# Two order edges behind a pair by seven products in a streaming-encoder block

## The chip, the cores and the metric

The kernel runs on one core of one Trainium2 chip. The metric is the device time of one execution in microseconds; several runs are taken, and their median is compared. Durations of single instructions come from one further, profiled execution.

## The reference

One layer of a hybrid encoder block on 256 rows of width 4096, all in float32, with every weight read once from memory:

```
xn   = rms_norm(x)
proj = xn @ w_in                      # 4096 x 14336: q, k, v, z_a, a_c, g_c, z_c
y_a  = rms_norm(chunked_attention(q, k, v)) * silu(z_a)
y_c  = rms_norm(conv_module(a_c, g_c)) * silu(z_c)     # gate, 31 taps, layer norm, @ w_pw
h    = x + concat(y_a, y_c) @ w_out                    # 4096 x 4096
gate = sigmoid(rms_norm(h) @ w_ple_gate + b_ple_gate)  # 4096 x 4096
out  = rms_norm(h + gate * (p @ w_ple))
```

Nearly all the work is in the matrix products with w_in, w_out and w_ple_gate.

## The kernel before, in words

**Parts.** TensorE (PE) multiplies values of a shortened float32 type. So each operand is split into a high part (`wh`, `uh`, `xh`: the value cast to that type) and a low part (`wl`, `ul`, `xl`: the value less its high part), and one product of float32 quality is three matmuls: xh by wh, xl by wh, xh by wl. For a weight, ScalarE (ACT) makes the cast (L204 in `parts_of`) and VectorE (DVE) the subtraction (L205 in the same helper).

**Tiles and loops.** `mixed_product` (L377) makes the product of all 256 rows (two halves of 128) with two column blocks of 512, in four accumulators. It goes through the weight's rows in blocks of 128, two at a time: a pair. An order, given as text (L348 to L362), lists the pairs and how each is done. A plain pair takes its two weights as they are, 24 matmuls. A pair marked `*` or `+` is done by seven products (P1 to P7) in place of eight, as in Strassen's scheme, 21 matmuls; it needs sums of weight blocks besides. With the weights w0 (first) and w1 (second) of the pair these are:

- the first sums `ua` (L518 and L519 on DVE; with `+` DMAs make them), with their cast and low part (`pair_parts`, L335, which calls `parts_of` and so shows as `uh` at L204 and `ul` at L205),
- the second sums `ub` (L531 and L532 on DVE, in that order, since the second needs the first), with their cast and low part too. P6 and P4 need these and are the last two in the list of products (L543 to L552).

The first weight of such a pair is split in its first column block alone (512 elements a partition, the rest 1024). In many orders the second sums are written over the first (`ua<-ua,wt` in the profile), in others to a tile of their own (`ub`). A mark `-` means that the second weight's low part is made by ACT's negated copy (L215 and L217 in `high_and_minus`) and an accumulating DMA of GpSimd (L524, or L495 in a plain pair); its products wait in a list until the next pair.

**Order.** Each engine works through its own queue strictly as written. The program is traced in the order of the source, and a planner then writes each engine's queue: it takes, by an estimate of times, the instruction that is first in the source among those whose inputs it expects to be there. An instruction of the following pair so gets in front of one of this pair that is not ready in the estimate. `pin` (L89) keeps marked instructions in the source's order. `queued_behind` (L223) opens a block in which each instruction on an engine gets an edge to a given instruction of that same engine: it is put later in the queue. No semaphore is involved. Before the change it is used in one place, L520, for the first sums of a pair marked `+`.

**Stages.** `mixed_product` is called 24 times: four times for the convolution's gated input (`glu_conv`, L802), six times for queries, keys and values (`heads`, L1021), twice for w_pw, four times for the output gates (`gated`, L1126), four times for w_out (L1215), and four times for the last gate with w_ple_gate (L1256 and L1302), which the text calls the gate products. Other work (attention, the convolution's taps, the layer norm) is laid between the pairs with `fill`.

Of the kernel before, what the change touches and what calls it, by code (L numbers as in the profile page):

```python
# [25 lines left out]
def hybrid_block(  # L26
# [72 lines left out]
    def two_columns(w, kb, col, apart):  # L99

        rows = w[kb * P : (kb + 1) * P, :]
        return bass.AP(
            tensor=rows.tensor, offset=rows.offset + col,
            ap=[list(rows.ap[0]), [apart, 2], [1, NB]],
        )
# [76 lines left out]
    def fill(n):  # L182
        for _ in range(min(n, len(later))):
            later.popleft()()
# [11 lines left out]
    def part_tiles():  # L196
        return [wpool.tile([P, KC, NB], F32R, tag=tag, name=tag, bufs=3) for tag in ("wh", "wl")]

    def parts_of(wt, kc, tiles=None):
        if tiles is None:  # L200
            tiles = part_tiles()
        wh, wl = tiles
        made = (
            nc.scalar.copy(wh[:, :kc, :], wt[:, :kc, :]),  # L204
            nc.vector.tensor_tensor(  # L205
                wl[:, :kc, :], wt[:, :kc, :], wh[:, :kc, :].bitcast(F32), ALU.subtract
            ),
        )
        recent[:] = made
        return (wh, wl), made  # L210

    def high_and_minus(wt):

        wh = wpool.tile([P, KC, NB], F32R, tag="wh", name="wh", bufs=3)
        nc.scalar.copy(wh, wt)  # L215
        low = spool.tile([P, KC, NB], F32R, tag="stage", name="low")
        nc.scalar.activation(low, wh.bitcast(F32), AF.Identity, scale=-1.0)  # L217
        return wh, low

    recent = []  # L220

    @contextmanager
    def queued_behind(made):  # L223

        with ExitStack() as queued:
            for ins in made:
                queued.enter_context(tc.issue_after(ins.ins))
            yield
# [106 lines left out]
    def pair_parts(src):  # L335

        tiles = [upool.tile([P, 2, NB], F32R, tag=tag, name=tag) for tag in ("uh", "ul")]
        return parts_of(src, 2, tiles)[0]
# [38 lines left out]
    def mixed_product(  # L377
# [37 lines left out]
        def add(name, x, w2, n, final, kinds=range(3), then=lambda ins: None):  # L415

            for kind in kinds:
                a, b = ((x[0], w2[0]), (x[1], w2[0]), (x[0], w2[1]))[kind]
                made.append(
                    nc.tensor.matmul(  # L420
                        banks[name], a, b, start=name not in begun,
                        stop=final and ends[name] == n and kind == 2 and not (left and name in "P2 P3 P4"),
                    )
                )
                begun.add(name)
                then(made[-1])

        def block(kb, h):
            t = lhs[kb // 4]
            return [t[:, kb % 4, q, h * P : (h + 1) * P] for q in range(2)]  # L430

        def add_plain(n, k, wh, wl, **kw):
            pair = order[n][0]
            for j in range(2):
                for h in range(NH):
                    name = (("P2", "P3"), ("P4", "X"))[h][j]
                    add(name, block(2 * pair + k, h), (wh[:, j], wl[:, j]), n, k == 1, **kw)

        waiting = []

        def add_waiting(n):

            while waiting and waiting[0][0] <= n:
                waiting.pop(0)[1]()
# [26 lines left out]
        for n, (pair, seven, by_dma) in enumerate(order):  # L471
            if n < done:
                continue
            if ahead:
                ahead(pair)
            wts = []
            for k in range(2):
                wt = wpool.tile([P, 2, NB], F32, tag="w", name="wt")
                if seven == "+" and k == 0:
                    nc.sync.dma_start(wt[:, 0], w[2 * pair * P : (2 * pair + 1) * P, col : col + NB])  # L480
                else:
                    nc.sync.dma_start(wt, two_columns(w, 2 * pair + k, col, apart))
                wts.append(wt)
            sums_ahead(n)
            if n >= len(order) - n_left:
                for k in range(2):
                    tiles = left[2 * (n - len(order) + n_left) + k]
                    held.append((2 * pair + k, parts_of(wts[k], 2, tiles and tiles())[0]))
                fill(fills[n % len(fills)])
                continue  # L490
            if not seven:
                add_plain(n, 0, *parts_of(wts[0], 2)[0])
                if by_dma:
                    wh, low = high_and_minus(wts[1])
                    nc.gpsimd.dma_start(  # L495
                        low, two_columns(w, 2 * pair + 1, col, apart), accum_op=ALU.add
                    )
                    add_plain(n, 1, wh, low, kinds=range(2))
                    waiting.append((n + 1, partial(add_plain, n, 1, wh, low, kinds=(2,))))
                else:  # L500
                    add_plain(n, 1, *parts_of(wts[1], 2)[0])
                add_waiting(n)
                fill(fills[n % len(fills)])
                continue
            begins = not helper
            if begins:
                for name in ("P1", "P5", "P7", "P6"):
                    helper[name] = ps_tmp.tile([P, NB], F32, tag="tmp", name=f"acc_{name}")
                banks.update(helper)
            w0, w1 = wts  # L510
            plus = partial(nc.vector.tensor_tensor, op=ALU.add)
            before = list(recent)
            w0h, w0l = parts_of(w0, 1)[0]
            if seven == "+":
                ua = ub = sums[n]
            else:
                ua = ub = upool.tile([P, 2, NB], F32, tag="u", name="ua")
                plus(ua[:, 0], w0[:, 0], w0[:, 1])  # L518
                plus(ua[:, 1], w0[:, 1], w1[:, 1])  # L519
            with queued_behind(before if seven == "+" else ()):  # L520
                uah, ual = pair_parts(ua)
            if by_dma:
                w1h, w1l = high_and_minus(w1)
                nc.gpsimd.dma_start(  # L524
                    w1l, two_columns(w, 2 * pair + 1, col, apart), accum_op=ALU.add
                )
            else:
                w1h, w1l = parts_of(w1, 2)[0]
            if seven == "*" and not sums:
                ub = upool.tile([P, 2, NB], F32, tag="u", name="ub")  # L530
            plus(ub[:, 0], ua[:, 0], w1[:, 1])  # L531
            plus(ub[:, 1], ub[:, 0], w1[:, 0])  # L532
            ubh, ubl = pair_parts(ub)
            first = len(made)

            def s_of(i):
                if pair in places:
                    return places[pair][i]
                t, at = comb[pair] if isinstance(comb, dict) else (comb[pair // 4], pair % 4)
                return [t[:, at + i // 2, q, (i % 2) * P : (i % 2 + 1) * P] for q in range(2)]  # L540

            k0, k1 = 2 * pair, 2 * pair + 1
            add("P1", block(k0, 0), (w0h[:, 0], w0l[:, 0]), n, True)  # L543
            add("P5", s_of(1), (uah[:, 0], ual[:, 0]), n, True)
            add("P7", s_of(0), (uah[:, 1], ual[:, 1]), n, True)
            for name, x, j in (("P2", block(k1, 0), 0), ("P3", s_of(3), 1)):
                part = partial(add, name, x, (w1h[:, j], w1l[:, j]), n, True)
                part(kinds=range(2 if by_dma else 3))
                if by_dma:
                    waiting.append((n + 1, partial(part, kinds=(2,))))  # L550
            add("P6", s_of(2), (ubh[:, 0], ubl[:, 0]), n, True)
            add("P4", block(k1, 1), (ubh[:, 1], ubl[:, 1]), n, True)  # L552
            add_waiting(n)
            if begins and on_begin:
                on_begin()
            if begins:
                tc.add_manual_dep(
                    made[first].ins, last_transpose[0].ins.name,
                    mybir.DependencyInfo(mybir.DependencyClass.NoSync, mybir.DependencyReason.DATA),
                    reason="transposes before the helpers take their banks",  # L560
                )
            if n == last_seven:
                on_helpers(helper)
                after_sevens()
            fill(fills[n % len(fills)])
# [859 lines left out]
```

## Time and profile before

| | before |
|---|---|
| median of 3 runs | 2026.0 us (2025.92 to 2027.42) |
| the profiled execution's own time | 2025.85 us |
| its span, first to last instruction | 2024.1 us |
| ACT busy | 1257.1 us (62%) |
| idle time of ACT before `wh` at L204, ended by PE | 351.7 us |
| idle time of ACT before `uh` at L204, ended by L532 | 76.1 us (39.2 for `ub`, 36.9 for `ua`) |
| weight loads by DMA, 512 KB each, issue to landing | 4.2 to 4.9 us |

A row of a timeline gives the start and the duration in us, the engine, the line of the kernel, the operation, the tile written and the tiles read, the shape, a count where equal instructions are merged, and in brackets the engine's idle time before it with what ended it. Starts of PE's matmuls are recorded, their ends are modelled. The granted clock of TensorE was 0.998 over the span.

### The profile page before, as it was taken

The numbers are of one execution on the slowest core, as the hardware profiler recorded it, in microseconds if no ns is written. First come the engines' busy times: TensorE is split into PE (matmuls) and PEld (weight loads), VectorE is DVE, ScalarE is ACT, GpSimd is POOL, SyncE is SP. The second block draws the span as 40 slices with busy tenths as digits, with TensorE's granted clock in tenths as the row PEclk, the third lists the DMA queues.
The fourth block names the chain that finished last, engine by engine and source line by source line (L and its number), as shares of the span: only waits on it lengthen the run. The fifth ranks groups of instructions, "written<-read, shape, count | busy, mean of one in ns | idle before, by whom it ended". The sixth has DMA issues, their size and how long they took to land.

```text
span 2024.1 us, 26329 instructions
## 1 busy us (share of the span) xinstructions
PE 2006.7 (99%) x9043; PEld 1648.0 (81%) x9043; DVE 1926.9 (95%) x2771; ACT 1257.1 (62%) x1634; POOL 65.3 (3%) x71
## 2 busy tenths in 40 slices
PE   9999999999999999999999999999999999999997
PEld 7888888878888888788888888887888888888876
DVE  7999999899999999888999999999999999999998
ACT  7655555665666556776566676765766766656565
POOL 0000000000000000000000000000000000000000
PEclk9999999999999999999999999999999999999999
DMA  8788878679668877556677786876767766666765
GB/s 290 225 233 241 249 221 250 178 220 257 200 198 257 255 206 235 164 176 205 202 239 215 225 244 209 240 239 204 236 215 230 234 200 200 211 218 206 232 207 180
DMA packets 174193, 447.72 MB, mean 221 GB/s; under 512 B 14302, under 2 KB 17518, under 8 KB 174058
## 3 DMA queue, kind: packets, MB, share of 16 engines
q1 hardware_dynamic: 161952, 417.93, 63.8%
q0 software_dynamic: 11456, 27.27, 7.9%
q8 instruction: 71, 1.16, 0.2%
q10 hardware_dynamic: 650, 0.84, 0.1%
q14 instruction: 64, 0.52, 0.1%
HBM read 441.78 MB, written 4.19 MB: 220 GB/s over the span
## 4 chain that ended last, share of the span: by engine, by line
PE 89%; DVE 6%; issue 2%; DMA 1%; ACT 1%; POOLq 0%; POOL 0%; ACTq 0%; DVEq 0%; SPq 0%
PE acc L420 68%; PE acc_P L420 17%; DVE wl L205 2%; DMA wt<-in_w_in_dram 1%; PE tmp_ps L170 1%; DVE cv L787 1%; PE acc L237 1%; DVE ul L205 1%; PE tmp_ps L959 0%; PE tmp_ps L943 0%; PE tmp_ps L977 0%; ACT uh L204 0%; DVE cv L868 0%; ACT wh L204 0%; PE tmp_ps L982 0%
## 5 line engine op out<-in xcount | busy, mean ns | idle before, releaser
L420 PE MATMUL acc<-wh,big_t 128*128 128x512 f32 x4028 | 1240.3, 391 | 0.9 <-ACT big_t L156 0.4
L204 ACT CAST wh<-wt 128x1024 fp32r<-128x1024 f32 (+1 forms) x716 | 684.3, 965 | 493.8 <-PE acc L420 351.7
L420 PEld LDWEIGHTS acc<-wh,big_t 128*128 128x128 f32 x4028 | 753.3, 188 | 157.1 <-issue 1.3
L205 DVE TENSOR_TENSOR wl<-wt,wh 128x1024 fp32r<-128x1024 f32 (+1 forms) x716 | 788.8, 1113 | 33.0 <-ACT wh L204 27.5
L420 PE MATMUL acc<-wl,big_t 128*128 128x512 f32 x1958 | 756.4, 392 | 0.3 <-DVE wl L205 0.2
L420 PEld LDWEIGHTS acc<-wl,big_t 128*128 128x128 f32 x1958 | 367.2, 188 | 78.1 <-DVE wl L205 2.7
L204 ACT CAST uh<-ua 128x1024 fp32r<-128x1024 f32 x187 | 196.6, 1051 | 103.0 <-DVE ua L519 51.7
L205 DVE TENSOR_TENSOR ul<-ua,uh 128x1024 fp32r<-128x1024 f32 x187 | 228.1, 1220 | 6.9 <-ACT uh L204 4.2
L787 DVE SCALAR_TENSOR_TENSOR cv<-uT,dw,cv 128x255 f32<-128x255 f32 (+23 forms) x480 | 203.6, 463 | 1.1
L420 PE MATMUL acc_P<-uh,big_t 128*128 128x512 f32 x570 | 174.6, 391 | 0.1
L204 ACT CAST uh<-ub 128x1024 fp32r<-128x1024 f32 x99 | 104.2, 1053 | 47.9 <-DVE ub L532 39.2
L420 PEld LDWEIGHTS acc_P<-uh,big_t 128*128 128x128 f32 x570 | 106.0, 188 | 24.5 <-ACT uh L204 3.3
L205 DVE TENSOR_TENSOR ul<-ub,uh 128x1024 fp32r<-128x1024 f32 x99 | 120.8, 1220 | 0.8 <-ACT uh L204 0.5
L420 PE MATMUL acc_P<-ul,big_t 128*128 128x512 f32 x285 | 109.7, 392 | 0.2 <-DVE ul L205 0.2
L420 PE MATMUL acc<-uh,big_t 128*128 128x512 f32 x286 | 88.6, 390 | 0.0
L420 PE MATMUL acc_P<-wh,big_t 128*128 128x512 f32 x286 | 88.3, 389 | 0.0
L518 DVE TENSOR_TENSOR ua<-wt 128x512 f32<-128x512 f32 x112 | 76.9, 686 | 10.0 <-DMA wt<-in_w_in_dram 6.2
L519 DVE TENSOR_TENSOR ua<-wt 128x512 f32<-128x512 f32 x112 | 76.8, 686 | 2.7 <-DMA wt<-in_w_in_dram 1.7
L420 PE MATMUL acc_P<-uh,comb_t 128*128 128x512 f32 x228 | 70.3, 391 | 0.3 <-ACT uh L204 0.2
L532 DVE TENSOR_TENSOR ub<-ub,wt 128x512 f32<-128x512 f32 x99 | 68.1, 688 | 1.4
L531 DVE TENSOR_TENSOR ub<-ua,wt 128x512 f32<-128x512 f32 x99 | 67.8, 685 | 0.0
L420 PEld LDWEIGHTS acc_P<-ul,big_t 128*128 128x128 f32 x285 | 53.3, 188 | 13.9 <-DVE ul L205 3.0
(254 smaller groups left out, 1631.0 us busy)
## 6 DMA issues: line engine op xcount, KB each, us to landing
wt<-in_w_in_dram SPq DMA_DIRECT2D x416, 512.0 KB, 4.7
wt<-in_w_out_dram SPq DMA_DIRECT2D x128, 512.0 KB, 4.5
wt<-in_w_ple_gate_dram SPq DMA_DIRECT2D x128, 512.0 KB, 4.2
wt<-in_w_pw_dram SPq DMA_DIRECT2D x32, 512.0 KB, 4.9
ua<-in_w_in_dram SPq DMA_DIRECT2D x31, 512.0 KB, 4.3
ua<-in_w_in_dram POOLq DMA_DIRECT2D x31, 512.0 KB, 8.8
wt<-in_w_in_dram SPq DMA_DIRECT2D x31, 256.0 KB, 2.8
low<-in_w_in_dram POOLq DMA_DIRECT2D x12, 512.0 KB, 8.2
```

The costliest lines, as they stand in the source:

```text
L170: nc.tensor.transpose(pt[:, i * T + h * P : i * T + (h + 1) * P], src[:, h, b] if len(src.shape) == 4 else src[:, h, b * P : (b + 1) * P], ...
L204: nc.scalar.copy(wh[:, :kc, :], wt[:, :kc, :]),
L205: nc.vector.tensor_tensor(wl[:, :kc, :], wt[:, :kc, :], wh[:, :kc, :].bitcast(F32), ALU.subtract),
L237: nc.tensor.matmul(acc, a, b[:, k, :], start=kb == 0 and kind == 0, stop=kb == kblocks - 1 and kind == 2,)
L420: nc.tensor.matmul(banks[name], a, b, start=name not in begun, stop=final and ends[name] == n and kind == 2 and not (left and name in "P2 ...
L518: plus(ua[:, 0], w0[:, 0], w0[:, 1])
L519: plus(ua[:, 1], w0[:, 1], w1[:, 1])
L531: plus(ub[:, 0], ua[:, 0], w1[:, 1])
L532: plus(ub[:, 1], ub[:, 0], w1[:, 0])
L787: nc.vector.scalar_tensor_tensor(cv[:, i, PAD - k :], uT[:, i, : T + k - PAD], dw[:, b, k : k + 1], cv[:, i, PAD - k :], ALU.mult, ALU.add,)
```

## The change

Each pair by seven products now leaves two instructions behind in a list, `last_sums`: the second of its second sums (L532) and ACT's cast of the second sums. The pair that follows in the same product takes them out. Its first weight is split in a block queued behind the first of them, which puts an edge on its low part (DVE); its second weight is split in a block queued behind the other one, which puts an edge on its cast (ACT), and on the negated copy where the pair has the mark `-`. The issue of GpSimd's DMA stays outside the block. The edges are the same for a plain pair and a pair by seven products; the last three pairs of the very last product (`left`) get none. No operation is added or taken away.

```
-        waiting = []
+        waiting, last_sums = [], []
...
-            wts = []
+            wts, second_sums, sum_cast = [], last_sums[:1], last_sums[1:]
+            last_sums.clear()
...
             if not seven:
-                add_plain(n, 0, *parts_of(wts[0], 2)[0])
+                with queued_behind(second_sums):
+                    both = parts_of(wts[0], 2)[0]
+                add_plain(n, 0, *both)
                 if by_dma:
-                    wh, low = high_and_minus(wts[1])
+                    with queued_behind(sum_cast):
+                        wh, low = high_and_minus(wts[1])
...
                 else:
-                    add_plain(n, 1, *parts_of(wts[1], 2)[0])
+                    with queued_behind(sum_cast):
+                        both = parts_of(wts[1], 2)[0]
+                    add_plain(n, 1, *both)
...
-            w0h, w0l = parts_of(w0, 1)[0]
+            with queued_behind(second_sums):
+                w0h, w0l = parts_of(w0, 1)[0]
...
+            with queued_behind(sum_cast):
+                w1h, w1l = high_and_minus(w1) if by_dma else parts_of(w1, 2)[0]
             if by_dma:
-                w1h, w1l = high_and_minus(w1)
                 nc.gpsimd.dma_start(
                     w1l, two_columns(w, 2 * pair + 1, col, apart), accum_op=ALU.add
                 )
-            else:
-                w1h, w1l = parts_of(w1, 2)[0]
...
             plus(ub[:, 0], ua[:, 0], w1[:, 1])
-            plus(ub[:, 1], ub[:, 0], w1[:, 0])
+            last_sums.append(plus(ub[:, 1], ub[:, 0], w1[:, 0]))
             ubh, ubl = pair_parts(ub)
+            last_sums.append(recent[0])
```

## The prediction

> **What bounds the kernel now.** I read the page first, then busy time by stretch, then the timelines of VectorE (DVE), ScalarE (ACT) and TensorE (PE) around the pairs by seven products. Two rows of the page and one of the view by stretch:
>
> ```profile
> span 2024.1 us, 26329 instructions
> ...
> PE 2006.7 (99%) x9043; PEld 1648.0 (81%) x9043; DVE 1926.9 (95%) x2771; ACT 1257.1 (62%) x1634; POOL 65.3 (3%) x71
> ```
>
> ```profile
> 60.00:1992.00 1932.00, 1929.07 (x8663) 1585.48 (x8662) 1858.94 (x2655) 1198.56 (x1522) 62.54 (x61) 1.00 0.72 221
> ```
>
> In the last row the second number is the length, then busy PE, PEld, DVE, ACT, POOL, the granted clock, and DMA. PE is idle for 17.4 us of the span, but for only 2.93 us of the 1932 us between the start and the last tail. A busy end is modelled, so I also count a late start: products in a row start 0.23 us apart (430.03 and 430.26 below), and what exceeds that is lost. The change can only win these losses back, where they hang on the chain that it touches.
>
> That chain belongs to one pair by seven products: first of the second sums (L531), second of them (L532), ACT's cast of both (`uh`), DVE's low part (`ul`), then the last two products, P6 and P4. The change puts two instructions of the following pair behind it: on DVE the first weight's low part behind L532, on ACT the second weight's cast behind the sums' cast. Where the queue already runs so, nothing moves. The view of line 532 counts the pairs:
>
> ```profile
> L532 DVE TENSOR_TENSOR ub<-ub,wt x99: 677/686/694, 64.6 to 1980.7; 128x512 f32<-128x512 f32 x99
> L532 DVE TENSOR_TENSOR ua<-ua,wt x44: 672/684/697, 115.0 to 870.0; 128x512 f32<-128x512 f32 x44
> ```
>
> That is 143 pairs. Going through the timelines, I find the second weight's cast ahead of the sums' cast after 27 of them; these are the first and the last of the 27 casts:
>
> ```profile
> 64.27 1.04 ACT L204 CAST wh<-wt 128x1024 fp32r<-128x1024 f32 x1
> ```
>
> ```profile
> 1978.97 1.04 ACT L204 CAST wh<-wt 128x1024 fp32r<-128x1024 f32 x1
> ```
>
> In only 6 of these is the low part ahead of L532 as well. 20 of the 27 lie after 1740 us, in the gate products. So 116 of 143 places have the order already.
>
> **The change part by part.** Place A, third GLU product, DVE, ACT, PE:
>
> ```profile
> 427.44 0.69 DVE L518 TENSOR_TENSOR ua<-wt 128x512 f32<-128x512 f32 x1 [1.01 <-DMA wt<-in_w_in_dram]
> 428.05 0.68 DVE L531 TENSOR_TENSOR ua<-ua,wt 128x512 f32<-128x512 f32 x1
> 428.65 1.22 DVE L205 TENSOR_TENSOR wl<-wt,wh 128x1024 fp32r<-128x1024 f32 x1
> 429.79 0.68 DVE L532 TENSOR_TENSOR ua<-ua,wt 128x512 f32<-128x512 f32 x1
> ```
>
> ```profile
> 427.51 1.06 ACT L204 CAST wh<-wt 128x1024 fp32r<-128x1024 f32 x1 [0.98 <-PE acc_P L420]
> 430.50 1.04 ACT L204 CAST uh<-ua 128x1024 fp32r<-128x1024 f32 x1 [1.94 <-DVE ua L532]
> ```
>
> ```profile
> 430.03 0.39 PE L420 MATMUL acc<-wl,comb_x 128*128 128x512 f32 x1
> 430.26 0.39 PE L420 MATMUL acc<-wh,big_t 128*128 128x512 f32 x1
> 431.60 0.73 PE L420 MATMUL acc_P<-uh,comb_x 128*128 128x512 f32 x2 [0.95 <-ACT uh L204]
> 432.17 0.63 PE L420 MATMUL acc<-uh,big_t 128*128 128x512 f32 x2
> ```
>
> The low part of the following weight stands between the two sums; the sums' cast starts 0.03 us after L532 ends (429.79 + 0.68), and P6 starts 0.06 us after the cast ends. From 430.26 to 432.17 are three starts: 1.91 less 3 x 0.23 is 1.22 us lost. With the edge L532 starts at 428.65 and ends at 429.33, the cast runs 429.36 to 430.40, and P6 can start at 430.46, before its turn at 430.49. So 1.22 us come back. The price: the low part ends at about 430.5 instead of 429.87; its product is in none of these rows and is after P6 in the pair's own order, so I take nothing. The moved cast starts about 2.8 us later (427.51 to about 430.3); ACT sat idle for 1.94 us in front of the sums' cast, which covers it. Behind it only later casts wait, and they were to start once the sums' cast was over in any case.
>
> Place B, the fourth GLU product, has the same order:
>
> ```profile
> 606.68 1.22 DVE L205 TENSOR_TENSOR wl<-wt,wh 128x1024 fp32r<-128x1024 f32 x1
> 607.82 0.69 DVE L532 TENSOR_TENSOR ua<-ua,wt 128x512 f32<-128x512 f32 x1
> ```
>
> ```profile
> 608.91 0.39 PE L420 MATMUL acc<-wh,big_t 128*128 128x512 f32 x1
> 609.64 0.73 PE L420 MATMUL acc_P<-uh,comb_x 128*128 128x512 f32 x2 [0.34 <-ACT uh L204]
> 610.21 0.40 PE L420 MATMUL acc<-uh,big_t 128*128 128x512 f32 x1
> ```
>
> 1.30 less 0.69 is 0.61 us lost. L532 at 606.68 puts P6 1.14 us earlier, at 608.50, before its turn at 609.14: all 0.61 come back.
>
> Place C, second output product, where the following pair's second weight goes by DMA, and only ACT's order is concerned:
>
> ```profile
> 1434.76 0.69 DVE L532 TENSOR_TENSOR ub<-ub,wt 128x512 f32<-128x512 f32 x1
> ```
>
> ```profile
> 1435.46 1.06 ACT L215 CAST wh<-wt 128x1024 fp32r<-128x1024 f32 x1 [0.98 <-PE acc_P L420]
> 1436.42 1.05 ACT L204 CAST uh<-ub 128x1024 fp32r<-128x1024 f32 x1
> ```
>
> ```profile
> 1438.62 0.39 PE L420 MATMUL acc<-uh,big_t 128*128 128x512 f32 x1
> 1438.98 0.50 PE L420 MATMUL acc_P<-ul,big_t 128*128 128x512 f32 x1
> 1439.32 0.40 PE L420 MATMUL acc<-uh,big_t 128*128 128x512 f32 x1
> ```
>
> The sums are done at 1435.45, but ACT takes the weight first. Exchanged, the sums' cast runs from 1435.48, 0.94 us earlier, and their low part `ul`, for which PE waits at 1438.98, can follow it. PE lost 0.70 less 2 x 0.23, 0.24 us; I take it all back. The two casts only swap, so the negated copy behind them, and GpSimd's accumulating DMA that it releases, start when they did before: nothing, and at most one cast (1.06 us) if they do not, on a transfer whose product is deferred to the next pair. No other queue's DMA is moved.
>
> Place D, last gate product, with both orders inverted and the opposite effect:
>
> ```profile
> 1956.55 1.22 DVE L205 TENSOR_TENSOR wl<-wt,wh 128x1024 fp32r<-128x1024 f32 x1
> 1957.68 0.68 DVE L532 TENSOR_TENSOR ub<-ub,wt 128x512 f32<-128x512 f32 x1
> ```
>
> ```profile
> 1952.37 1.04 ACT L204 CAST wh<-wt 128x1024 fp32r<-128x1024 f32 x1
> ...
> 1958.47 1.05 ACT L204 CAST uh<-ub 128x1024 fp32r<-128x1024 f32 x1 [2.80 <-DVE ub L532]
> ```
>
> ```profile
> 1957.28 0.61 PE L420 MATMUL acc_P<-wh,big_t 128*128 128x512 f32 x2
> 1957.82 0.96 PE L420 MATMUL acc<-wl,big_t 128*128 128x512 f32 x3
> 1958.62 0.62 PE L420 MATMUL acc<-wh,big_t 128*128 128x512 f32 x2
> ```
>
> Here PE fills its time with the following pair: at 1957.82 it waits for exactly the low part that the change sends back (five starts in 1.34 us: 0.19 lost). After the change L532 takes 1956.55 to 1957.23 and the low part ends near 1958.4; the sums' cast is over at 1958.3, so the earliest product is P6 at 1958.35 in place of 1957.82: 0.5 us more. And the products with `wh` at 1958.62, of a cast made five microseconds before, now have it at 1959.3; P6 and P4 fill that time. Bounds: the 0.19 won, 0.5 lost; I take 0.2 lost, since PE's order is planned anew too. The gate product before has a place of this kind; I give it the same as an estimate. The other 22 places I set at nothing: some close a short loss, some lose a filler of PE as in D. Their bounds I put at 1.5 us either way in all, eight times the 0.19 of place D, as an estimate.
>
> Sum: 1.22 + 0.61 + 0.24 - 2 x 0.2 = 1.7 us. The profiled execution took 2025.85 us, 1.75 beyond its span; less 1.7 that is 2024.15. The median of the runs shown, 2026.0, is 0.15 above that execution, so the forecast for the median is 2024.3. That is 0.08%, under the 0.2% (4.05 us) that a measurement of this kernel can tell from no change.
>
> **The rivals.** *VectorE takes the gain back.* Won time is only kept if DVE follows:
>
> ```profile
> 432.00:540.00 108.00, 108.00 (x489) 89.01 (x488) 105.66 (x168) 61.78 (x74) 7.61 (x7) 1.00 0.87 251
> 1740.00:1916.00 176.00, 175.95 (x771) 143.55 (x770) 174.54 (x213) 106.11 (x128) 0.00 (x0) 1.00 0.67 214
> ```
>
> After place A, DVE is busy for 105.66 of 108 us: 2.34 us of slack for 1.22 us won, enough if it lies in the right place. In the gate products it is 1.46 us in 176. The change removes no DVE work, so if DVE binds, the sum is 0 and the median 2026.0. For it: these rows; against: at A it is DVE's order, not its amount, that PE waits for. The Trainium skill ("Perfetto Trace Analysis", Identifying the Most-Contended Engine) says that matmul busy time does not show how near PE is to its limit, and has it judged by the weight loads' busy share; by that rule PE has a fifth to spare and DVE is the bound, which gives this rival's time. The trace speaks against the rule here: products start every 0.23 us without a gap at 81% of weight loads.
>
> *The planner's new order closes more.* One early shift moves everything planned behind it; if every idle stretch of the 2.93 us closed, and as much again in late starts, it would be 5.9 us and 2020.1. For it: 27 places are spread over the kernel. Against: transposes and attention, which the change does not touch, share in that idle time.
>
> *Slower: loads come later.* Place A's first row shows DVE waiting 1.01 us for a weight's DMA; a weight buffer is free only once its cast and low part are done. A second cast that comes a cast later (1.06 us) frees it later; where no margin is left, DVE and then PE pay the 1.06. It decides from two such places on (2.1 against 1.7 won); with six of the 27 it is 6.4 - 1.7 = 4.7 us, 2030.7. Against: the low part, not the cast, is the last to read, and DVE's total is unchanged.
>
> *It does nothing*: the edges bind in none but the 27 places, and PE's order may absorb those too: 2026.0.
>
> **How the numbers follow.** Forecast (some 1 to 3 us won) 0.55; given back 0.17; nothing done 0.05; more closed 0.13; slower 0.10. Of the third, 0.10 lies beyond 4.05 us; of the fourth, 0.07. So faster 0.10, same 0.83, slower 0.07. The range goes from 2021.3 (1.5 from the unsized places and another 1.5 of replanning) to 2027.5 (the gain gone and 1.5 lost): about one in ten on either side.
>
> **What would show it.** Right: at A and B no idle time before `acc_P<-uh,comb_x`, with L532 straight behind L531 or after a sum; at C the cast `uh` ahead of L215; in no place a `wh` of the second weight ahead of the `uh`; ACT idle before `uh`, as long as before. Wrong: new PE waits after 1740 us for `wl` or `wh` of more than 0.5 us each, more DVE idle time at L518 that a weight's DMA ends, as place A's first row has it, or a span shorter by over 4 us, which would need places that I took for untouched.

## The result and the profile after

The changed kernel is slower by 0.15%, where a gain of 0.08% was forecast: median 2029.66 us (2027.06 to 2032.15, 22 runs) beside 2026.37 us of the kernel before (22 runs), ratio 1.0015, 95% interval 1.0008 to 1.0021. That is 1.6 to 4.3 us, near the least that such a comparison can tell from no change. Timed a second time, it gave 1.0013 (1.0004 to 1.0022). The profiled execution took 2028.23 us, 1.83 beyond its span. Of the later kernels, one run each of e5 (4338.92 us) and e8 (2222.42 us) was in a slow state and is left out of the ratios; all other runs are fast ones.

The page of the changed kernel, then its busy time by stretch (columns as in the prediction):

```profile
span 2026.4 us, 26338 instructions
...
PE 2006.3 (99%) x9043; PEld 1648.5 (81%) x9043; DVE 1927.4 (95%) x2771; ACT 1256.1 (62%) x1634; POOL 65.3 (3%) x71
```

```profile
60.00:1992.00 1932.00, 1926.80 (x8655) 1584.59 (x8654) 1858.40 (x2653) 1196.25 (x1521) 62.55 (x61) 1.00 0.72 220
...
1740.00:1916.00 176.00, 175.07 (x766) 142.83 (x765) 173.65 (x212) 105.41 (x127) 0.00 (x0) 1.00 0.67 213
```

The work is the same: 9043 products, 2771 instructions of DVE, equal busy times. PE's idle time between the start and the last tail grew from 2.93 to 5.20 us, and in the gate products (1740 to 1916) from 0.05 to 0.93. Eight products fewer fell into the first stretch, eight times 0.23 us.

For all later comparisons I sum PE's late starts over the whole trace: each start less the one before it, less the 0.2275 us of products in a row. Only excesses of more than about 0.02 us count, and a constant 5.5 us or so is in every sum; so differences of the sums are to be read, not the sums. The sum is 29.23 us before and 32.03 after. In every profile of this study the span is 1994.4 to 1995.0 us plus this sum, so it accounts for the difference of two spans to within 0.6 us: here the sums differ by 2.80 and the spans by 2.3.

**Place A after.** DVE, then PE. In this kernel the first sums are L525 and L526, the second sums L537 and L538 (before: L518, L519, L531, L532).

```profile
426.51 0.69 DVE L525 TENSOR_TENSOR ua<-wt 128x512 f32<-128x512 f32 x1 [0.76 <-DMA wt<-in_w_in_dram]
427.12 0.68 DVE L537 TENSOR_TENSOR ua<-ua,wt 128x512 f32<-128x512 f32 x1
427.80 0.69 DVE L526 TENSOR_TENSOR ua<-wt 128x512 f32<-128x512 f32 x1
428.41 0.69 DVE L538 TENSOR_TENSOR ua<-ua,wt 128x512 f32<-128x512 f32 x1
429.01 1.22 DVE L205 TENSOR_TENSOR wl<-wt,wh 128x1024 fp32r<-128x1024 f32 x1
```

```profile
429.36 0.39 PE L420 MATMUL acc<-wl,comb_x 128*128 128x512 f32 x1
430.28 0.72 PE L420 MATMUL acc_P<-uh,comb_x 128*128 128x512 f32 x2 [0.53 <-ACT uh L204]
430.85 0.63 PE L420 MATMUL acc<-uh,big_t 128*128 128x512 f32 x2
431.54 0.50 PE L420 MATMUL acc_P<-ul,comb_x 128*128 128x512 f32 x1
431.88 0.39 PE L420 MATMUL acc<-ul,big_t 128*128 128x512 f32 x1
```

The edge was obeyed: the low part `wl` stands behind L538. But L538 does not start at L537's end. The planner put L526 there, the second first sum of a later pair. And PE lost the filler `acc<-wh,big_t` that stood ahead of P6 at 430.26 before. From 429.36 to 431.88 are six starts: 2.52 less 6 x 0.23 is 1.14 us lost, against 1.22 before.

**Place B after**, DVE and PE:

```profile
606.50 0.69 DVE L526 TENSOR_TENSOR ua<-wt 128x512 f32<-128x512 f32 x1 [0.16 <-DMA wt<-in_w_in_dram]
607.11 0.69 DVE L538 TENSOR_TENSOR ua<-ua,wt 128x512 f32<-128x512 f32 x1
```

```profile
607.84 0.39 PE L420 MATMUL acc<-wl,comb_x 128*128 128x512 f32 x1
608.98 0.74 PE L420 MATMUL acc_P<-uh,comb_x 128*128 128x512 f32 x2 [0.76 <-ACT uh L204]
...
610.58 0.39 PE L420 MATMUL acc<-ul,big_t 128*128 128x512 f32 x1
```

The same newcomer, and it waits for its weight's DMA. Six starts in 2.74 us: 1.36 us lost, where 0.61 were to be won.

**Place C after**, ACT, then PE:

```profile
1437.07 1.05 ACT L204 CAST uh<-ub 128x1024 fp32r<-128x1024 f32 x1 [1.09 <-DVE ub L538]
1438.03 1.04 ACT L215 CAST wh<-wt 128x1024 fp32r<-128x1024 f32 x1
```

```profile
1439.67 0.62 PE L420 MATMUL acc_P<-uh,big_t 128*128 128x512 f32 x2
1440.12 0.39 PE L420 MATMUL acc_P<-ul,big_t 128*128 128x512 f32 x1
1440.35 0.62 PE L420 MATMUL acc<-uh,big_t 128*128 128x512 f32 x2
```

The two casts have changed places, and three starts in 0.68 us leave nothing lost.

**Place D after**, the last gate product, DVE, ACT and PE:

```profile
1956.04 0.68 DVE L537 TENSOR_TENSOR ub<-ua,wt 128x512 f32<-128x512 f32 x1
1956.64 1.21 DVE L205 TENSOR_TENSOR ul<-ua,uh 128x1024 fp32r<-128x1024 f32 x1
1957.77 0.68 DVE L538 TENSOR_TENSOR ub<-ub,wt 128x512 f32<-128x512 f32 x1
1958.38 1.21 DVE L205 TENSOR_TENSOR wl<-wt,wh 128x1024 fp32r<-128x1024 f32 x1
```

```profile
1958.56 1.05 ACT L204 CAST uh<-ub 128x1024 fp32r<-128x1024 f32 x1 [2.44 <-DVE ub L538]
```

```profile
1958.80 0.39 PE L420 MATMUL acc<-wh,big_t 128*128 128x512 f32 x1
1959.67 0.74 PE L420 MATMUL acc_P<-uh,big_t 128*128 128x512 f32 x2 [0.48 <-ACT uh L204]
1960.25 0.63 PE L420 MATMUL acc<-uh,big_t 128*128 128x512 f32 x2
1960.72 0.85 PE L420 MATMUL acc<-wl,big_t 128*128 128x512 f32 x3
```

L538 is not earlier here: this time the low part `ul` of the first sums took the freed place. P6 starts at about the time at which it did before (1959.77), but PE runs dry ahead of it: before, ten products with weights of following pairs stood between 1957.28 and P6, and now most of these are planned behind it, as the `wl` at 1960.72. Three starts in 1.45 us: 0.76 lost. The view of PE's waits from 1740 us on (us in all, times, the longest) shows it for the gate products as a whole:

```profile
PE acc_P L420 <- ACT uh L204: 1.4, 3, 0.5
PE acc L408 <- DVE wl L205: 0.5, 1, 0.5
```

Three waits, one in each of the last three gate products, and one at the start of the last product's remainder at 1994.67; the kernel before has no wait of PE in this window.

### The profile page after: what moved, and what is told of

Its sections match the earlier page's. It is cut to its first block, busy times and chain, and to the rows that moved or that the text cites. A ratio compares the mean times of both kernels' runs of the same rounds, so it can differ in the third digit from the quotient of the medians.

```text
span 2026.4 us, 26338 instructions
## 1 busy us (share of the span) xinstructions
PE 2006.3 (99%) x9043; PEld 1648.5 (81%) x9043; DVE 1927.4 (95%) x2771; ACT 1256.1 (62%) x1634; POOL 65.3 (3%) x71
## 4 chain that ended last, share of the span: by engine, by line
PE 86%; DVE 7%; issue 3%; DMA 2%; ACT 1%; SPq 0%; POOLq 0%; POOL 0%; ACTq 0%; DVEq 0%
PE acc L420 65%; PE acc_P L420 17%; DVE wl L205 3%; DMA wt<-in_w_in_dram 1%; DVE ul L205 1%; PE tmp_ps L170 1%; PE acc L237 1%; DVE cv L794 1%; ACT uh L204 0%; ACT wh L204 0%; DVE hc L184 0%; DVE ua L525 0%; DVE ub L537 0%; PE tmp_ps L966 0%; PE tmp_ps L950 0%
## 5 line engine op out<-in xcount | busy, mean ns | idle before, releaser
L525 DVE TENSOR_TENSOR ua<-wt 128x512 f32<-128x512 f32 x112 | 76.6, 684 | 9.4 <-DMA wt<-in_w_in_dram 5.8
L526 DVE TENSOR_TENSOR ua<-wt 128x512 f32<-128x512 f32 x112 | 76.6, 684 | 4.6 <-DMA wt<-in_w_in_dram 4.1
L538 DVE TENSOR_TENSOR ub<-ub,wt 128x512 f32<-128x512 f32 x99 | 68.0, 687 | 1.5
L537 DVE TENSOR_TENSOR ub<-ua,wt 128x512 f32<-128x512 f32 x99 | 67.6, 682 | 0.0
```

Of the source, the lines that this page charges most:

```text
L538: last_sums.append(plus(ub[:, 1], ub[:, 0], w1[:, 0]))
```

## The experiments

The late starts of all profiles, in us, beside medians of 11 runs where nothing else is said (the GLU products named are the third and fourth, with places A and B; the gate products are the last four):

| kernel | median | ratio (95% interval) | two GLU | gate | rest | sum |
|---|---|---|---|---|---|---|
| before (3 runs) | 2026.0 | | 9.15 | 3.48 | 16.61 | 29.23 |
| e12 before again | 2025.58 | 0.9999 (0.9991 to 1.0008) | 8.58 | 3.41 | 16.76 | 28.75 |
| after (22 runs) | 2029.66 | 1.0015 (1.0008 to 1.0021) | 9.16 | 5.10 | 17.77 | 32.03 |
| e13 after again | 2028.92 | 1.0013 (1.0004 to 1.0022) | 9.41 | 4.93 | 18.23 | 32.57 |
| e1 low part alone | 2027.31 | 1.0007 (0.9998 to 1.0016) | 8.79 | 4.28 | 17.18 | 30.25 |
| e2 cast alone | 2028.93 | 1.0010 (1.0001 to 1.0019) | 10.02 | 5.51 | 17.54 | 33.07 |
| e3 gate products alone | 2027.67 | 1.0001 (0.9992 to 1.0010) | 8.73 | 5.14 | 15.85 | 29.73 |
| e4 all but gate products | 2027.62 | 1.0003 (0.9994 to 1.0012) | 10.02 | 3.54 | 17.54 | 31.11 |
| e5 first sums too | 2025.65 | 0.9999 (0.9990 to 1.0008) | 7.21 | 5.58 | 15.72 | 28.51 |
| e6 two GLU products | 2025.15 | 0.9995 (0.9986 to 1.0004) | 7.36 | 3.41 | 16.94 | 27.70 |
| e7 three places | 2028.52 | 1.0011 (1.0003 to 1.0020) | 9.49 | 5.92 | 15.16 | 30.57 |
| e8 all but three places | 2028.08 | 1.0009 (1.0000 to 1.0018) | 12.57 | 2.39 | 17.12 | 32.09 |
| e9 first sums too, but three | 2023.63 | 0.9990 (0.9981 to 0.9999) | 7.28 | 2.43 | 18.26 | 27.98 |
| e10 two GLU and gate | 2024.28 | 0.9990 (0.9981 to 0.9999) | 8.08 | 2.44 | 16.82 | 27.34 |
| e11 first sums, later P6 | 2024.56 | 0.9996 (0.9987 to 1.0005) | 7.13 | 3.57 | 16.31 | 27.01 |
| e14 first sums alone | 2025.48 | 0.9993 (0.9984 to 1.0001) | 7.40 | 3.45 | 16.80 | 27.65 |
| e15 TensorE's order alone (5 runs) | 2033.76 | 1.0040 (1.0026 to 1.0053) | 9.33 | 10.50 | 16.31 | 36.14 |
| e16 middle alone | 2025.60 | 0.9996 (0.9988 to 1.0005) | 8.21 | 3.28 | 17.35 | 28.84 |

A ratio is to runs of the kernel before made beside that kernel, and it is not the quotient of two medians: e3's median is 1.7 us over that of the runs beside it (2025.99), at a ratio of 1.0001. The late starts are those of a single execution each.

**Halves of the change (e1 to e4).** One edge at a time, then both edges in one part of the kernel. e1 and e2:

```
-            wts, second_sums, sum_cast = [], last_sums[:1], last_sums[1:]
+            wts, second_sums, sum_cast = [], last_sums[:1], []
...
+            wts, second_sums, sum_cast = [], [], last_sums[1:]
```

> Only the edge on VectorE is kept (the following first weight's low part behind L532); the cast on ScalarE is free. Theory 1, the loss comes from the gate products, where the second cast may no longer come early and TensorE is planned without its fillers: the low part stood ahead of L532 in 6 places only, so within 1 us of the kernel before (2025.5 to 2027.5 where before is 2026.4). Theory 2, the loss comes from the low part moved back, for which TensorE waits, and from the sums of other pairs that take its place: most of the 3.3 us, 2028.5 to 2030.

> Only the edge on ScalarE is kept (the following second cast behind the cast of the sums). Theory 1: nearly the whole loss stays, 2 to 3.5 us over before, with waits of 0.6 us for the cast of the sums in the last three gate products. Theory 2: under 1 us over before.

e3 and e4, where `products_made` counts the calls of `mixed_product`:

```
+            if len(products_made) <= 20:
+                second_sums, sum_cast = [], []
...
+            if len(products_made) > 20:
+                second_sums, sum_cast = [], []
```

> Both edges in the four gate products alone. Theory 1: 1.8 us over before, what TensorE lost there in the profile after (4.45 us of late starts after 1740 us against 2.66). Theory 3, the loss is at the boundaries of products (the four output gates), where the plan came out otherwise by chance: within 0.7 us of before.

> Both edges everywhere but in the gate products. Theory 1: 0.5 to 1.5 us over before, from the boundaries of the output gates; the third and fourth GLU product gain nothing together. Theory 3: 2.5 to 3.5 us over before.

By time the four can't be told apart: their intervals overlap, and e1, e3 and e4 hold 1. The traces say more. Each edge alone makes new waits before P6 in the last two gate products (e1: 0.67 and 0.64 us idle; e2: 0.48 and 0.44), and e2 makes the third as well (0.45); so the loss there is not that of one of the edges alone. And e3, with the edges in the gate products alone, has all of their extra late starts (5.14), e4 none (3.54). In e3's own time this loss does not show (1.0001, 0.9992 to 1.0010).

**The first sums at A and B (e5, e6, e14).** Here the first sums of a pair are queued behind the preceding pair's second sums as well. In e5 that is added to the change everywhere; in e6 only the low-part edge and this one stay, in the two GLU products alone.

```
+                with queued_behind(second_last):
                     plus(ua[:, 0], w0[:, 0], w0[:, 1])
                     plus(ua[:, 1], w0[:, 1], w1[:, 1])
...
             last_sums.append(recent[0])
+            second_last[:] = last_sums[:1]
```

> The change, and besides it the first sums of each later pair by seven (L518, L519) queued behind the last second sums in the same product. Theory 1: in the third and fourth GLU product the freed place between L531 and L532 was taken by such a sum, which waits for its weight's DMA; with this edge L532 follows L531 there, the product P6 waits less than 0.3 us (0.69 to 1.45 and 0.41 to 0.92 in the profiles with the change), and the kernel is 1.5 to 2.5 us under the change, 0.5 to 1.5 over before. Rival, VectorE takes the gain back: the waits close and the time stays that of the change.

> The low part's edge and the edge on first sums in the third and fourth GLU product alone, no edge on a cast, nothing elsewhere. Theory 1: both waits for P6 (1.22 and 0.61 us lost before) go, 1 to 2 us under before. Rival, VectorE takes the gain back: within 0.5 us of before, with later waits in the attention that follows.

The waits before P6 are gone in both, at A and at B. PE of e5 at A:

```profile
429.00 0.61 PE L420 MATMUL acc_P<-uh,comb_x 128*128 128x512 f32 x2
429.55 0.50 PE L420 MATMUL acc_P<-ul,comb_x 128*128 128x512 f32 x1
429.89 0.64 PE L420 MATMUL acc<-uh,big_t 128*128 128x512 f32 x2
```

P6 follows the product before it without idle time, and three starts in 0.89 us leave 0.20 lost, not 1.14. At B a wait for the sums' low part `ul`, just behind, took the place of the one before P6. PE of e6 at B:

```profile
608.96 0.50 PE L422 MATMUL acc_P<-ul,comb_x 128*128 128x512 f32 x1 [0.25 <-DVE ul L205]
```

B loses 0.43 us in e5 and 0.52 in e6, where the two profiles of the kernel before lose 0.61 and 0.47: no gain beyond what these two differ by. Over the whole kernel e5 is level with the kernel before, e6 not clear of it (0.9995, to 1.0004), and e5's median is 4 us under that of the change (from different comparisons).

e14 then took the low-part edge away and left the kernel before with the first-sum edge alone, in these two products:

```
+            second_sums, sum_cast = [], []
+            if len(products_made) not in (5, 7):
+                second_last.clear()
```

> The kernel before with one edge only: in the third and fourth GLU products the first sums (L518, L519) are queued behind the second of the second sums; the low part and the cast are free. Theory 1 (the low part still stands between the two sums, and both edges are needed): a wait of 0.5 to 1.3 us before P6 at about 430 us and 0.2 to 0.6 at about 608 us, as in the kernel before, and the time within 1 us of it. Rival (the first sums alone are the cause): no wait at either place, and 1 to 2 us under the kernel before.

I expected that both edges were needed. At A that was wrong. DVE of e14, whose second sums are L543 and L544, and PE:

```profile
424.46 1.23 DVE L205 TENSOR_TENSOR ul<-ua,uh 128x1024 fp32r<-128x1024 f32 x1
425.72 0.69 DVE L543 TENSOR_TENSOR ua<-ua,wt 128x512 f32<-128x512 f32 x1
426.33 1.22 DVE L205 TENSOR_TENSOR wl<-wt,wh 128x1024 fp32r<-128x1024 f32 x1
427.47 0.68 DVE L544 TENSOR_TENSOR ua<-ua,wt 128x512 f32<-128x512 f32 x1
```

```profile
429.30 0.39 PE L421 MATMUL acc<-wl,comb_x 128*128 128x512 f32 x1
429.52 0.62 PE L421 MATMUL acc_P<-uh,comb_x 128*128 128x512 f32 x2
```

The low part still stands between the two second sums, and P6 is on time. What also held the chain up at A is in the first row that the prediction quotes of this place: the first sum at 427.44, ahead of the second sums, with 1.01 us of idle time for its weight's DMA. It belongs to a later pair, whose weight was not there; without it the first of the second sums starts 0.03 us after the work before it. Taking it out is enough: A loses 0.31 us in e14. Whether moving the low part alone would have been enough too, with nothing in its place, no run shows. At B, where that first sum had not waited, e14 still has 0.27 us idle before P6, and the kernels with the low-part edge besides (e5, e6, e9, e10) have none. There P6 did wait for the low part, as predicted, but the place loses as much with `ul` late. The two GLU products lose 7.40 us in e14 and 7.21 and 7.36 in e5 and e6; so nearly all that is won there is won at A, and by the first sums.

**The gate products (e7, e8, e11, e15).** e7 leaves both edges only behind the pair `6*` of the last three gate products; e8 takes out just these.

```
+            if not (len(products_made) > 21 and n == 7):
+                second_sums, sum_cast = [], []
...
+            if len(products_made) > 21 and n == 7:
+                second_sums, sum_cast = [], []
```

> Both edges behind one pair by seven in each of the last three gate products alone (the pair after which two of the low parts and all three casts stood ahead): 3 of the 143 places. Theory 1: P6 waits 0.6 us at each, 1.0 to 1.8 us over before in the profile's late starts. Rival, the gate products lose by all 20 of their places together: under 0.5 us.

> The change without these three places. Theory 1: the waits of 0.6 us in the gate products go, 1.0 to 1.8 us under the change, about 1.5 to 2 over before. Rival: as the change.

The three places alone bring the waits (5.92 us in the gate products) and, by time, a ratio of 1.0011 (1.0003 to 1.0020). Without them the gate products are better than before, 2.39 us. That e8 as a whole is not faster than the kernel before (1.0009) may come from its GLU products, 12.57 us in its profiled execution, where the wait before P6 at A was 1.81 us; of its other executions there is no trace.

e7 shows one thing more. DVE, then PE, in the gate product before the last:

```profile
1866.68 0.69 DVE L542 TENSOR_TENSOR ub<-ua,wt 128x512 f32<-128x512 f32 x1
1867.40 0.69 DVE L543 TENSOR_TENSOR ub<-ub,wt 128x512 f32<-128x512 f32 x1
```

```profile
1869.30 0.74 PE L422 MATMUL acc_P<-uh,big_t 128*128 128x512 f32 x2 [1.18 <-ACT uh L204]
```

Here nothing stands between the second sums (L542 and L543 in this kernel), as the prediction had it, and P6 still waits 1.18 us, longer than in the changed kernel. It is the same in the last product. So the loss in the gate products does not need the taken place.

Which engine's order does it? e11 keeps all of e5's edges on DVE and ACT and only writes P6 and P4 of that pair behind the products of the following first weight in the source:

```
                 add_plain(n, 0, *both)
+                while later_two:
+                    later_two.pop()()
...
-            add("P6", s_of(2), (ubh[:, 0], ubl[:, 0]), n, True)
-            add("P4", block(k1, 1), (ubh[:, 1], ubl[:, 1]), n, True)
...
+            if len(products_made) > 21 and n == 6:
+                later_two.append(last_two)
+            else:
+                last_two()
```

> The change with the first sums also queued behind the second sums, and with P6 and P4 of the pair 6* in the last three gate products written behind the two products of the following first weight, so that the planner has fillers for TensorE ahead of P6. All VectorE and ScalarE edges of the change stay. Theory 1 (the gate products lose since TensorE has nothing planned ahead of P6): the waits of 0.6 us before P6 at about 1780, 1868 and 1957 us are gone or below 0.2 each, and the time is 1 to 2 us under the version with the first sums alone (2025.65), 2023.7 to 2024.7. Rival (the sums' chain itself runs too late on VectorE and ScalarE): the waits of 0.6 us stay or move to the products behind, and the time stays at 2025 to 2026.

e15 does the opposite to the kernel before: no edge on DVE or ACT, but PE's products of that first weight queued behind P4.

```
-                add_plain(n, 0, *parts_of(wts[0], 2)[0])
+                both = parts_of(wts[0], 2)[0]
+                with queued_behind(last_p4 if len(products_made) > 21 and n == 7 else ()):
+                    add_plain(n, 0, *both)
...
+            last_p4[:] = made[-1:]
```

> The kernel before with no edge on VectorE or ScalarE; in the last three gate products TensorE's products of the first weight behind the pair 6* are queued behind the pair's P4. Theory 1 (TensorE's lost fillers alone make the new waits): waits of 0.5 to 1.2 us before P6 at about 1780, 1869 and 1957 us, and 1 to 3 us over the kernel before, ratio 1.0005 to 1.0015. Rival (VectorE's and ScalarE's order makes them): no wait over 0.2 us there, and the time of the kernel before.

PE of e11, then of e15:

```profile
1955.75 0.50 PE L422 MATMUL acc_P<-uh,big_t 128*128 128x512 f32 x1 [0.24 <-ACT uh L204]
1956.08 1.08 PE L422 MATMUL acc<-wl,big_t 128*128 128x512 f32 x4
```

```profile
1960.50 0.62 PE L421 MATMUL acc_P<-ul,big_t 128*128 128x512 f32 x2
1962.07 0.73 PE L421 MATMUL acc_P<-uh,big_t 128*128 128x512 f32 x2 [0.95 <-ACT uh L204]
```

e15 alone makes waits of 0.93 to 0.95 us before P6 in all three products, a further 1.08 us for `ul`, and costs 0.4%: 7.0 us of late starts in the gate products, more than twice what I had expected. In e11 four products `wl` run right behind the first one of P6; of its three waits one is gone and two are halved (0.24 idle), 3.57 against 5.58 us of late starts in the gate products. At the three places themselves 2.2 us become 1.3; the rest lies elsewhere, above all at a wait for `ul` at 1752 that e5 has and e11 has not and at the last product's remainder. So PE's order is enough to make this loss, and mending it alone takes a good part of it away, with the sums' chain in the same order on DVE and ACT. By time e11 (0.9996) and e5 (0.9999) can't be told apart.

**Putting it together (e9, e10).** e9 is e5 without the three gate places. e10 has the low-part and first-sum edges in the two GLU products, the gate products as in e9, and nothing between.

```
+            if len(products_made) in (5, 7):
+                sum_cast = []
+            elif len(products_made) <= 20:
+                second_sums, sum_cast, second_last[:] = [], [], []
+            if len(products_made) > 21 and n == 7:
+                second_sums, sum_cast = [], []
```

> The change with two additions: the first sums of the pair after next (L518, L519) are also queued behind the second of the second sums, and both of the change's edges are off behind the pair 6* of the last three gate products. Theory 1 (the change loses its time at two kinds of place: in the GLU products a first sum that waits for its weight's DMA takes the place that was freed, and in the last three gate products TensorE's fillers are planned behind P6): no wait of TensorE before P6 at about 429 and 608 us, none of 0.6 us at about 1780, 1868 and 1957 us, and the time 2 to 4 us under the kernel before, 2022 to 2024, ratio 0.998 to 0.999, 4 to 6 us under the change alone. Rival (each order edge wins at one place what the planner loses at another): waits of the same sum elsewhere, the time within 1 us of the kernel before, ratio 0.9995 to 1.0005.

> Only the places where the runs so far showed a gain: in the third and fourth GLU products the low part behind the second sums and the first sums behind them too; in the gate products the change without the place behind the pair 6* of the last three. Everything between is the kernel before. Theory 1: no wait before P6 at about 429 and 608 us, none of 0.6 us in the gate products, and 2 to 3 us under the kernel before, 2023 to 2024, ratio 0.9985 to 0.999; if also the diffuse loss of the change between 610 and 1740 us is real, 1 to 2 us better than with the edges in all products. Rival (the planner's chance): within 1 us of the kernel before.

Both beat both kernels, at the weak end of what was expected (e10 0.3 us beyond it): ratio 0.9990 (0.9981 to 0.9999) to the kernel before, 2023.63 and 2024.28 us. The intervals end just below 1. That the edges between the GLU and the gate products cost something was not borne out: e9, which has them, is no slower than e10.

**The controls and what lies between (e12, e13, e16).** The two kernels once more, unchanged, and the change from the 8th to the 20th product alone:

```
+            if not 8 <= len(products_made) <= 20:
+                second_sums, sum_cast = [], []
```

> The kernel before once more, as a control: ratio 1.000 within 0.001. It shows how much the waits at the two GLU places and the late starts of TensorE differ from one profiled execution to another of the same program. Theory 1: the wait before P6 at about 431 us between 0.8 and 1.5 us, at about 609 us between 0.4 and 0.9, the span within 1.5 us of 2024.1. Rival (the differences between these kernels' profiles are no more than such a spread): waits at these places from 0 to over 1.5 us, and a span 2 to 3 us away.

> The changed kernel once more, as a control. If the loss is the program's own: ratio 1.0015 within 0.0009, waits of 0.4 to 0.5 us before P6 at about 1782, 1871 and 1959 us as before, and waits for the gate's sums (z) between 1000 and 1300 us of over 1 us in all. Rival (those waits for z belong to one execution): under 0.5 us of them in this one.

> The change in the products between the GLU and the gate products alone (about 640 to 1740 us). If the edges cause the spread loss: late starts of TensorE 1 us more there than in the kernel before, and 0.5 to 2 us over it, ratio 1.0003 to 1.001. Rival (it is the difference between executions): ratio 1.000 within the interval, and late starts there between 2.5 and 4.4 us, as in the profiles of the kernel before.

The kernel before again, DVE and PE, then the changed kernel again, DVE and PE, at A:

```profile
426.21 0.69 DVE L518 TENSOR_TENSOR ua<-wt 128x512 f32<-128x512 f32 x1 [1.25 <-DMA wt<-in_w_in_dram]
```

```profile
430.38 0.73 PE L420 MATMUL acc_P<-uh,comb_x 128*128 128x512 f32 x2 [1.19 <-ACT uh L204]
```

```profile
428.49 0.69 DVE L526 TENSOR_TENSOR ua<-wt 128x512 f32<-128x512 f32 x1 [0.59 <-DMA wt<-in_w_in_dram]
```

```profile
430.97 0.72 PE L420 MATMUL acc_P<-uh,comb_x 128*128 128x512 f32 x2 [1.28 <-ACT uh L204]
```

In this execution the newcomer L526 waits 0.59 us between the two second sums, and P6 1.28 us: more than in either profile of the kernel before. At B the kernel before waited less than expected in e12, 0.20 us. The gate products repeat to 0.2 us. The waits for the output gates' sums `z`, which I had suspected, do not: 1.6 us in three waits after, 1.0 in e13, 0.3 in one before, 0.9 in e12. And e16 is not slower than the kernel before; its late starts outside the GLU and gate products, 17.35 us, are 0.6 to 0.7 over both profiles of that kernel, which settles neither theory.

## Why the prediction was wrong

**The step that failed** is "With the edge L532 starts at 428.65". It took the place that the edge freed for the sum's own. An edge says only what may not stand there; the planner filled it with the next instruction that it expected to be ready, L526 in the GLU products and `ul` in the gate products. At A and B 1.83 us were to come back. The two profiles of the changed kernel lose 9.16 and 9.41 us in these two products, the two of the kernel before 9.15 and 8.58: nothing came back. In the gate products a second step failed, the bound of 0.5 us lost at D: it left out that PE's fillers would be planned behind P6.

**The cause at A was read in part.** "The low part of the following weight stands between the two sums" is what the rows show. They also show a first sum ahead of both, held by a DMA, and e14 shows that moving this one is enough. At B the reading of the wait was right, and the price was not: e5 and e6 close the wait before P6, and the 0.61 us do not come back, since `ul` is then waited for (0.43 and 0.52 us lost, against 0.61 and 0.47 in the kernel before).

**Place D and its twin** were thought of, with the right sign and for part of the right reason ("some lose a filler of PE as in D"), but at 0.2 us each, and not for the gate product before those. The steps allowed P6 at 1958.35 on the premise that L532 moved up; in the changed kernel it did not. In e7 it did, P6 started at 1958.27, and PE had waited 1.18 us for it, with its fillers planned behind. Measured, the gate products lose 1.5 to 1.6 us more (5.10 against 3.48; again 4.93 against 3.41): three waits of P6 and one for `wl` of 0.53 us (0.42 in e13) in the last product's remainder, at 1994.67, where the prediction priced nothing; among its signs of being wrong it names such a wait. 0.5 us each as the worst case was too narrow since PE's new order was left out of the bound: e15 shows 2.3 us a place when PE's products of the following first weight all go behind P4.

**Place C** went as predicted, in its mechanism and its size. The nine profiles without the cast's edge there (before, e1, e3, e6, e7, e10, e12, e14, e15) lose 0.24 us at that place, the nine with it (after, e2, e4, e5, e8, e9, e11, e13, e16) nothing. It is too little to show in a time.

**The sum.** Of about 3 us measured, 1.5 to 1.6 are the gate products, shown by the traces of e3, e7, e8, e11 and e15, and by time in e7 and e15. The two GLU products add 0 to 0.8 by these profiles. The rest of the kernel adds 1.2 to 1.5 in after and e13 over before and e12, but it lies between 15.2 and 18.3 us in all the profiles, it is highest in the fastest kernel (e9), and e16 has no loss. This part stays open: it may be the edges in connection with the earlier places, or DMAs that land at other times.

**The rivals.** *VectorE takes the gain back* is refuted, as far as times just clear of noise can do it: e9 and e10 have the same DVE work (2771 instructions, 1926.1 and 1926.5 us busy), closed waits of PE and are faster than the kernel before. e5, e6 and e14, with the waits at A closed, have spans 0.4 to 1.6 us under the two profiles of the kernel before, but by time they can't be told from it. The Trainium skill ("Perfetto Trace Analysis", Identifying the Most-Contended Engine) judges PE's headroom by MFU (the share of its peak rate, not worked out here) and the weight loads' busy share. The latter, 81%, leaves a fifth to spare, and that was not borne out here: products start every 0.2275 us, and fewer late starts made a faster kernel. *Loads come later*, the rival with the right sign, had another mechanism than the one that came: DVE's idle time at first sums that wait for blocks of w_in, 7.9 us before and 10.7 in e12, is 9.9 after and 10.9 in e13, no difference beyond that of two executions.

## What to carry to other kernels

An edge that forbids one instruction a place in an engine's queue does not give that place to the one that you want: look what is next in line, on every engine that the planner orders anew, and price the loss of a filler in front of a dependent product (here 0.7 to 0.8 us late at each place, 0.4 to 0.6 more than before) as well as the wait that is to go. When a wait is gone, look for the one just behind it: at B it lost as much. When a chain is late, start at its first row: an instruction of other work that waits for a DMA in front of the chain holds up all that is queued behind it, as at A. Moving those first sums, and leaving the fillers of PE alone, made of the same idea a kernel that is 0.1% faster than before (e9 and e10, ratio 0.9981 to 0.9999).

## What the runs showed of the hardware

One program differs from execution to execution by more than the effect: e12's 11 runs went from 2024.32 to 2028.38 us at a granted clock of 0.998. When weights land is one thing that differs: the same first sum at A waited 1.01 us in one profile of the kernel before and 1.25 in another. The wait of P6 behind it was 0.95 and 1.19 us. How much of the spread this makes the runs do not show.
